# Attention's value products moved from one tile of keys to two behind the transposes, and a block's output split by ScalarE and VectorE out of PSUM

## The chip, the cores and the metric

The kernel runs on one core of a Trainium2 chip. The metric is the device time of one execution in microseconds. Three runs of the kernel before took 2472.91, 2474.02 and 2474.15 us; the median is 2474.02 us. A profiled execution is one run of its own.

Engines are named as in the profile: PE is TensorE's matmul, PEld its weight load, DVE is VectorE, ACT is ScalarE, POOL is GpSimd, and SP the engine whose queue issues nearly all DMAs.

## The reference, cut to what matters

The model has two layers at a width of 1024 on 1024 tokens, all in float32. Layer 0 mixes by attention, layer 1 by an mLSTM, and each is followed by a SwiGLU feed-forward network. The change touches layer 0's attention alone:

```python
h = h + nsa_swa_mixer(rmsnorm(h, norm_mix[0]), ...)   # 8 NSA heads and 8 sliding-window heads, 2 key heads each
# for each block of 128 queries, NSA (gates g0, g1, g2 per head):
p_c = masked_softmax(q @ kc.T * scale, ...)    # 63 compressed keys
p_s = masked_softmax(q @ ksel.T * scale, ...)  # top 16 of 16 key blocks of 64: all causal keys here
p_w = masked_softmax(q @ kwin.T * scale, ...)  # the last 512 keys
o_a = g0 * (p_c @ vc) + g1 * (p_s @ vsel) + g2 * (p_w @ vwin)
# sliding window with sinks, span of 256 keys:
e = exp(logits - max(logits.max(), sink));  p = e / (e.sum() + exp(sink - max))
o_b = p @ v
out = concat(o_a, o_b) @ w_out
```

## The kernel before

A float32 product is made of two parts that TensorE takes, `hi` (the value cast to fp32r) and `lo` (what is left). A dense product is three matmuls per 128x128 weight: hi by hi, hi by lo, lo by hi (lines 188 to 190 while attention runs). Splitting a tile costs one cast (ACT or POOL) and one subtraction (DVE).

**Blocks.** Attention runs over 32 blocks. A block is one kind (1: window with sinks, 0: NSA), one key head g (4 query heads share it) and one tile n of 128 queries. First come the 16 sink blocks, then 16 NSA blocks, n from 0 to 3 for either g, then 4 to 7. A sink block has one unit of work; an NSA block has three: the compressed keys, the n+1 tiles of selected keys, and up to 5 tiles of the window.

**A unit** passes through three steps, each one unit behind the one before, in `blocks()`: `scores` (line 592; queries times keys into PSUM tile S, then mask and maximum by DVE on line 643, then the exponential by ACT on line 652 into tile e), `weights` (line 665; POOL scales e by gate over sum, line 684), and `values` (line 686). So while unit i's scores are made, unit i-2's values are.

**Values.** For each tile of 128 keys, PE transposes four 128x128 pieces of e into a PSUM tile T (line 701), ACT casts T into `eh` (line 705), DVE subtracts to get the low part `el` (line 706, shown as eh too), and PE multiplies both by the values into the block's accumulator `po` (lines 695 and 696). The values sit as hi and lo side by side in the 128 columns of the stationary operand, so `po` holds the hi product in partitions 0 to 63 and the lo product in 64 to 127. `late` holds the products of one tile back until the next tile's transposes have been issued. The last tile's products of a unit are made at the start of the next unit's loop.

**Output.** `outputs()` (line 713) copies `po` out of PSUM by ACT (`oc`, line 716), and POOL makes three instructions of it: the hi part of the upper half (line 117), the rest of it (line 720) and that plus the lower half (line 721). Two DMAs store both parts to `os` in DRAM (line 724).

**Order.** The Tile layer schedules each engine's queue by its own model and inserts the semaphores. `pinned` keeps an instruction behind all that was traced before it on its engine; the first transpose of a tile and both products are pinned. Each engine runs its queue in order. A tile tag with `bufs` names at most so many live tiles; the packer then gives each tile an address, and a tile may reuse the address of any dead one, of another tag too. A new tile waits for the last readers of what lay there, DMAs included.

**Dense work beside.** A list `beside` in `mixer_ab` gives generators of dense products (the rest of the input projection, then the output projection `ab_out`), each with a position at which its loads are issued and a stretch of positions over which its steps are spread. A position is the number of the block and the share of it that has been traced. `ab_out` reads back what `outputs()` stored.

After block 31 the last quarter of the output projection and the first two tiles of the feed-forward network (`ffn_head`) follow, then a chain of vector work that makes the operands of the big feed-forward products.

```python
ec = self.page("w", "ec", w=256)                       # 625
eh, el = self.pair("k", "eh")                          # 704
if late: products(*late)                               # 707
c = self.page("w", "oc"); t = self.page("w", "ot"); o = self.page("w", "o", F32R)   # 715 to 718
```

Of the kernel before, what the change touches and what calls it, by code (L numbers as in the profile page):

```python
# [20 lines left out]
OP = mybir.AluOpType  # L21
# [15 lines left out]
class Net:  # L37
# [554 lines left out]
    def scores(self, q, unit, g, n):  # L592
# [21 lines left out]
        if br == 0:  # L614
            p = tile()
            for r in range(4):
                products(p, 64 * r, r)
            yield st, es
            s = p[:, :256].rearrange("p (r k) -> p r k", r=4)
            nc.vector.tensor_tensor(s, s, mask[:, None, :].to_broadcast([P, 4, 64]), op=OP.add)  # L620
            nc.vector.tensor_reduce(nm, s, AX.X, OP.max, negate=True)
            if n == 0:

                nc.vector.tensor_scalar(nm, nm, 1e20, None, op0=OP.min)
            ec = self.page("w", "ec", w=256).rearrange("p (r k) -> p r k", r=4)
            for r in range(4):
                nc.scalar.activation(ec[:, r], s[:, r], AF.Exp, bias=nm[:, r:r + 1], accum_out=l[:, r:r + 1])
                es.append(ec[:, r])
            yield st, es
            return  # L630
# [52 lines left out]
        for r in range(4):  # L683
            self.last_scale = nc.gpsimd.tensor_scalar(es[r][:, :w], es[r][:, :w], f[:, r:r + 1], 0.0, op0=OP.mult, op1=OP.add)  # L684

    def values(self, unit, es, po, first, last):


        nc = self.nc
        br, _, w, _, vals = unit  # L690
        n = min(P, w)
        late = None

        def products(j, v, eh, el):
            self.pinned(nc.tensor.matmul(po, v[:n], eh[:n], start=first and j == 0, stop=False))  # L695
            self.pinned(nc.tensor.matmul(po, v[:n], el[:n], start=False, stop=last and j == len(vals) - 1))  # L696

        for j, v in enumerate(vals):
            tp = self.tmp_ps("T")
            for r in range(4):  # L700
                t = nc.tensor.transpose(tp[:n, r * P:(r + 1) * P], es[r][:, j * P:j * P + n], self.ident)  # L701
                if r == 0:
                    self.pinned(t)
            eh, el = self.pair("k", "eh")
            nc.scalar.copy(eh[:n], tp[:n])  # L705
            nc.vector.tensor_tensor(el[:n], tp[:n], eh[:n].bitcast(F32), op=OP.subtract)  # L706
            if late:
                products(*late)
            late = j, v, eh, el
            yield  # L710
        yield lambda: products(*late)

    def outputs(self, kind, g, n, po):
        nc = self.nc
        c = self.page("w", "oc")
        nc.scalar.copy(c, po)  # L716
        t = self.page("w", "ot")
        o = self.page("w", "o", F32R)
        self.hi_copy(o[0:64], c[0:64], "pool")
        nc.gpsimd.tensor_tensor(t[64:128], c[0:64], o[0:64].bitcast(F32), op=OP.subtract)  # L720
        nc.gpsimd.tensor_tensor(o[64:128], c[64:128], t[64:128], op=OP.add)
        r0 = (kind * 8 + 4 * g) * 64
        for i in range(2):
            nc.sync.dma_start(self.os[i, r0:r0 + 256, n * P:(n + 1) * P].rearrange("(r d) q -> d r q", d=64),
                              o[64 * i:64 * i + 64].bitcast(F32).rearrange("d (r q) -> d r q", r=4))

    def blocks(self, todo):
# [7 lines left out]
                work.append((b, k, k == len(sizes) - 1))  # L735
                pos.append((i + sum(sizes[:k]) / sum(sizes), size / sum(sizes)))
        pos += [(len(todo) + i, 1) for i in range(2)]
        qs, done, late = {}, [], None

        def ahead(i):  # L740
            if i < len(todo):
# [4 lines left out]
        for i in range(len(work) + 2):  # L746
            tiles, sc = iter(()), iter(())
            per = 1
            if i > 1:
                b, k, last = work[i - 2]  # L750
                unit = done[i - 2][2]
                if k == 0:
                    po = self.acc("po")
                tiles = self.values(unit, done[i - 2][1], po, k == 0, last)
                per = -(-len(unit[4]) // 4)
            if i < len(work):
                b, j, _ = work[i]
# [4 lines left out]
            if 0 < i <= len(work):  # L762
                st, es, u = done[i - 1]
                self.weights(u, work[i - 1][0][1], work[i - 1][0][2], st, es)
            res, end = None, None
            self.attn = "sinks" if pos[i][0] < 24 else "nsa"
            for r in range(5):
                res = next(sc, res)
                if r == 0 and late:
                    late()  # L770
                    late = None
                for k in range(per):
                    x = next(tiles, None)
                    if callable(x):
                        end = x
                    yield pos[i][0] + pos[i][1] * (r * per + k + 1) / (5 * per)
            for x in tiles:
                if callable(x):
                    end = x
            for res in sc:  # L780
                pass
            if i < len(work):
                done.append((*res, us[j]))
            if end:
                def late(end=end, args=work[i - 2][0], po=po, last=work[i - 2][2]):
                    end()
                    if last:
                        self.outputs(*args, po)
        late()

    def mixer_ab(self):
        nc, tc = self.nc, self.tc
# [2 lines left out]
        with tc.tile_pool(name="at", bufs=1) as self.at:  # L795
# [21 lines left out]
            def parts():  # L817
                for c in range(NC):
                    with self.tc.issue_after(self.last_scale.ins):
# [4 lines left out]
            beside = [(0.0, 0.0, 13.6, 80, second), (14.0, 14.0, 17.8, 16, third),  # L824
                      (18.0, 18.6, 26.4, 32, self.ab_out(range(4, 8), (0, 1))),
                      (26.9, 27.8, 31.0, 17, squares(self.ab_out(range(0, 4), (0,)))),
                      (31.8, 32.4, 33.9, 9, self.ab_out(range(0, 2), (1,))), (32.4, 32.4, 33.9, 8, parts())]
            done = [0] * len(beside)
            for at in self.blocks(todo):
                for i, (load, start, end, steps, gen) in enumerate(beside):  # L830
# [768 lines left out]
```

## Time and profile before

| | |
|---|---|
| runs shown, median (lowest to highest) | 2474.02 us (2472.91 to 2474.15) |
| the profiled execution: its own time, its span | 2475.77 us, 2474.00 us |
| PE busy | 2374.9 us, 96% |
| DVE, ACT, POOL busy | 1630.4 us (66%), 896.7 us (36%), 501.9 us (20%) |
| TensorE's granted clock, mean | 0.982 |
| first transposes of e for values, last `po` product | 100.1 us, 649.8 us |

The span is what the profile covers; 1.77 us of the execution's own time lie outside it. Attention with the dense work beside it fills about 80 to 650 us of the span. A matmul's end is modelled, so PE counts as busy in part of a wait; a weight load (PEld) is issued for each matmul ahead of it, and a wait for an operand shows on PEld first. The granted clock is the share of full speed (2.4 GHz; the other level is 1.2 GHz) over a stretch.

### The profile page before, as it was taken

How to read it: one execution, taken by the hardware profiler on the slowest of the kernel's cores; microseconds unless marked ns; L12 is line 12 of the kernel's file. 1: busy time of each engine (PE TensorE's matmuls, PEld its weight loads, DVE VectorE, ACT ScalarE, POOL GpSimd, SP SyncE). 2: the span in 40 equal slices, each digit the busy share in tenths (PEclk: the TensorE clock that was granted, in tenths of full speed). 3: DMA queues.
4: the chain of work that ended last, by engine and by line, in shares of the span. 5: the costliest groups of instructions: out<-in, count | busy, mean ns of one | idle time of the engine just before them, and what ended most of it. 6: DMA issues, size and time to landing. Idle time of an engine off the chain costs nothing.

```text
span 2474.0 us, 29578 instructions
## 1 busy us (share of the span) xinstructions
PE 2374.9 (96%) x10729; PEld 1895.6 (77%) x10729; DVE 1630.4 (66%) x2817; ACT 896.7 (36%) x1851; POOL 501.9 (20%) x606
## 2 busy tenths in 40 slices
PE   7999998998889999999999999999979999999998
PEld 5778776776668888887777788887868888887886
DVE  6546666688786666668876554544487656667867
ACT  5234565576353223222222344332263222322222
POOL 3135654444300000002322111111100000002322
PEclk9999999999989999999999999999989999999999
DMA  5623642311434443449333211112143434348433
GB/s 190 196 69 111 199 123 60 89 45 37 136 99 139 134 132 124 155 152 323 127 134 101 65 43 39 39 56 102 40 144 107 154 108 165 128 162 300 139 140 115
DMA packets 246757, 304.20 MB, mean 123 GB/s; under 512 B 19076, under 2 KB 157524, under 8 KB 246612
## 3 DMA queue, kind: packets, MB, share of 16 engines
q1 hardware_dynamic: 246612, 302.31, 37.8%
q8 instruction: 85, 1.39, 0.2%
q14 instruction: 60, 0.49, 0.1%
HBM read 218.33 MB, written 83.90 MB: 122 GB/s over the span
## 4 chain that ended last, share of the span: by engine, by line
PE 67%; DVE 6%; issue 4%; POOL 4%; ACT 2%; DMA 1%; SPq 0%; DVEq 0%; POOLq 0%; ACTq 0%
PE dn L1173 14%; PE wb L993 10%; PE wb L994 10%; PE wb L995 10%; PE acc L181 4%; PE acc L180 4%; PE acc L179 4%; POOL e L684 1%; PE T L701 1%; PE S L610 1%; DVE y L124 1%; POOL x L245 1%; PE po L695 1%; PE po L696 1%; PE pr L995 1%
## 5 line engine op out<-in xcount | busy, mean ns | idle before, releaser
L993 PE MATMUL wb<-y,wh 128*128 128x512 f32 x1120 | 442.6, 395 | 6.1 <-ACT wh L119 4.8
L994 PE MATMUL wb<-y,wh 128*128 128x512 f32 x1120 | 442.7, 395 | 0.0
L995 PE MATMUL wb<-y,wh 128*128 128x512 f32 x1120 | 441.0, 394 | 0.0
L117 POOL TENSOR_SCALAR wo<-ws 128x1024 fp32r<-128x1024 f32 x84 | 121.3, 1456 | 1099.2 <-DVE m L1061 437.7
L993 PEld LDWEIGHTS wb<-y,wh 128*128 128x128 f32 x1120 | 210.8, 188 | 58.8 <-ACT wh L119 5.2
L995 PEld LDWEIGHTS wb<-y,wh 128*128 128x128 f32 x1120 | 211.1, 188 | 49.7 <-DVE wh L124 0.7
L994 PEld LDWEIGHTS wb<-y,wh 128*128 128x128 f32 x1120 | 210.9, 188 | 48.1
L1173 PE MATMUL dn<-xo,wo 128*128 128x512 f32 x924 | 220.1, 400 | 6.6 <-DVE wo L124 6.1
L1173 PE MATMUL dn<-wo,xo 128*128 128x512 f32 x924 | 215.7, 395 | 0.6 <-ACT xo L119 0.3
L1173 PEld LDWEIGHTS dn<-xo,wo 128*128 128x128 f32 x924 | 176.7, 192 | 49.9 <-DVE wo L124 7.4
L1173 PEld LDWEIGHTS dn<-wo,xo 128*128 128x128 f32 x924 | 173.7, 188 | 42.5 <-DVE xo L124 1.1
L179 PE MATMUL acc<-x,whl 128*128 128x512 f32 x416 | 170.1, 409 | 0.0
L180 PE MATMUL acc<-x,whl 128*128 128x512 f32 x416 | 166.1, 399 | 0.0
L181 PE MATMUL acc<-x,whl 128*128 128x512 f32 x416 | 165.3, 397 | 0.0
L188 PE MATMUL acc<-x,whl 128*128 128x512 f32 x384 | 157.6, 410 | 4.6 <-DMA x<-os 2.5
L684 POOL TENSOR_SCALAR e<-e,st 128x256 f32<-128x256 f32 (+7 forms) x192 | 122.2, 656 | 173.2 <-ACT oc L716 33.4
L189 PE MATMUL acc<-x,whl 128*128 128x512 f32 x384 | 155.1, 404 | 1.9 <-DVE x L246 1.0
L119 ACT CAST xo<-hb 128x1024 fp32r<-128x1024 f32 x84 | 79.4, 976 | 206.0 <-PE dn L1173 134.8
L190 PE MATMUL acc<-x,whl 128*128 128x512 f32 x384 | 153.2, 399 | 0.7 <-DVE whl L124 0.7
L706 DVE TENSOR_TENSOR eh<-T,eh 128x512 fp32r<-128x512 f32 (+1 forms) x178 | 120.3, 687 | 44.8 <-ACT eh L705 43.6
L124 DVE TENSOR_TENSOR wh<-ws,wh 128x512 fp32r<-128x512 f32 x136 | 92.8, 686 | 83.6 <-ACT wh L119 83.5
L610 PE MATMUL S<-kv,qa 128*128 128x256 f32 (+3 forms) x528 | 123.8, 331 | 11.5 <-ACT e L652 3.8
(334 smaller groups left out, 4415.8 us busy)
## 6 DMA issues: line engine op xcount, KB each, us to landing
ws<-in_ffn_w_down SPq DMA_DIRECT2D x34, 1024.0 KB
ws<-in_ffn_w_gate SPq DMA_DIRECT2D x22, 1024.0 KB
ws<-in_ffn_w_up SPq DMA_DIRECT2D x22, 1024.0 KB
sd<-m SPq DMA_DIRECT2D x22, 1024.0 KB
hs<-m SPq DMA_DIRECT2D x80, 256.0 KB
qa<-qs SPq DMA_DIRECT2D x128, 128.0 KB
hb<-hs SPq DMA_DIRECT2D x16, 1024.0 KB
ws<-sd SPq DMA_DIRECT2D x16, 1024.0 KB
```

The lines of the kernel that those rows point to most:

```text
L179: nc.tensor.matmul(ps, w[:, 0, k], xh, start=(start and k == 0), stop=False)
L180: nc.tensor.matmul(ps, w[:, 0, k], xl, start=False, stop=False)
L181: nc.tensor.matmul(ps, w[:, 1, k], xh, start=False, stop=(stop and k == n - 1))
L188: self.nc.tensor.matmul(ps, w[:, 0, i], xh, start=i == 0, stop=False)
L189: self.nc.tensor.matmul(ps, w[:, 0, i], xl, start=False, stop=False)
L190: self.nc.tensor.matmul(ps, w[:, 1, i], xh, start=False, stop=i == len(xs) - 1)
L610: nc.tensor.matmul(p[:, at + c:at + c + k.shape[1]], qq[:, r * P:(r + 1) * P], k, start=i == 0, stop=i == 1, skip_group_check=True)
L684: self.last_scale = nc.gpsimd.tensor_scalar(es[r][:, :w], es[r][:, :w], f[:, r:r + 1], 0.0, op0=OP.mult, op1=OP.add)
L993: nc.tensor.matmul(ps, t[:, 0, k], xh, start=first and k == 0, stop=False, skip_group_check=True)
L994: nc.tensor.matmul(ps, t[:, 0, k], xl, start=False, stop=False, skip_group_check=True)
L995: nc.tensor.matmul(ps, t[:, 1, k], xh, start=False, stop=last and k == 3, skip_group_check=True)
L1173: nc.tensor.matmul(ps[i], l, r, start=first and k == 0 and q == 0, stop=end and k == 10 and q == 2, skip_group_check=True)
```

## The change

`values` no longer keeps the products back itself. It puts each tile's products on a list `pending` that belongs to all of attention, and once more than two are on it, the oldest is made. So the products stand two tiles of keys behind the transposes, and the distance holds across units and blocks. `outputs` is called when a block's last product is made, and what is on the list at the end is made after the loop.

`outputs` reads `po` in PSUM directly: ACT casts the upper half to `o`, DVE subtracts that from the upper half, and DVE adds the lower half. POOL has no part in it, and `oc` is gone.

The tiles change place: `eh` and `el` become one tile of a tag of their own with 6 bufs, which the output's `o` and `t` share; `ec` moves to the tag `e`. One position in `beside` changes from 31.8 to 32.3.

```diff
-            ec = self.page("w", "ec", w=256).rearrange("p (r k) -> p r k", r=4)
+            ec = self.pg.tile([P, 2 * PAGE], F32, name="ec", tag="e", bufs=EB)[:, :256].rearrange("p (r k) -> p r k", r=4)
...
-    def values(self, unit, es, po, first, last):
+    def values(self, unit, es, po, first, last, pending, after):
...
             self.pinned(nc.tensor.matmul(po, v[:n], el[:n], start=False, stop=last and j == len(vals) - 1))
+            if last and j == len(vals) - 1:
+                after()
...
-            eh, el = self.pair("k", "eh")
+            t = self.pg.tile([P, 2, PAGE], F32R, name="eh", tag="eh", bufs=6)
+            eh, el = t[:, 0, :H5], t[:, 1, :H5]
             nc.scalar.copy(eh[:n], tp[:n])
             nc.vector.tensor_tensor(el[:n], tp[:n], eh[:n].bitcast(F32), op=OP.subtract)
-            if late:
-                products(*late)
-            late = j, v, eh, el
+            pending.append(lambda j=j, v=v, eh=eh, el=el: products(j, v, eh, el))
+            if len(pending) > 2:
+                pending.pop(0)()
             yield
-        yield lambda: products(*late)

     def outputs(self, kind, g, n, po):
         nc = self.nc
-        c = self.page("w", "oc")
-        nc.scalar.copy(c, po)
-        t = self.page("w", "ot")
-        o = self.page("w", "o", F32R)
-        self.hi_copy(o[0:64], c[0:64], "pool")
-        nc.gpsimd.tensor_tensor(t[64:128], c[0:64], o[0:64].bitcast(F32), op=OP.subtract)
-        nc.gpsimd.tensor_tensor(o[64:128], c[64:128], t[64:128], op=OP.add)
+        t = self.pg.tile([P, 2, PAGE], F32R, name="ot", tag="eh", bufs=6)
+        o, t = t[:, 0, :H5], t[:, 1, :H5].bitcast(F32)
+        nc.scalar.copy(o[0:64], po[0:64])
+        nc.vector.tensor_tensor(t[64:128], po[0:64], o[0:64].bitcast(F32), op=OP.subtract)
+        nc.vector.tensor_tensor(o[64:128], po[64:128], t[64:128], op=OP.add)
...
-                tiles = self.values(unit, done[i - 2][1], po, k == 0, last)
+                tiles = self.values(unit, done[i - 2][1], po, k == 0, last, pending, lambda b=b, po=po: self.outputs(*b, po))
...
-        late()
+        for late in pending:
+            late()
...
-                      (31.8, 32.4, 33.9, 9, self.ab_out(range(0, 2), (1,))), (32.4, 32.4, 33.9, 8, parts())]
+                      (32.3, 32.4, 33.9, 9, self.ab_out(range(0, 2), (1,))), (32.4, 32.4, 33.9, 8, parts())]
```

PE's order in NSA block 24 (kind 0, g = 0, n = 4), kernel before. `T_4151`, whose parts are `eh_4156` and `eh_4157`, is the tile transposed before `T_4167`:

```order
L701 MATMUL T_4167<-consts_80,e_4049 128x128
L610 MATMUL S_4207<-kv_1428,qa_3719 128x512
L695 MATMUL po_4058<-eh_4156,kv_1431 128x512
L610 MATMUL S_4207<-kv_1428,qa_3719 128x512
L610 MATMUL S_4207<-kv_1428,qa_3719 128x128 x2
L696 MATMUL po_4058<-eh_4157,kv_1431 128x512
L701 MATMUL T_4178<-consts_80,e_3989 128x128
```

The same place in the changed kernel. `eh_4007` comes from the tile two before `T_4035`, `eh_4030` from the one after that; lines 702, 694 and 695 are 701, 695 and 696 of before:

```order
L702 MATMUL T_4035<-consts_80,e_3912 128x128
L694 MATMUL po_3921<-eh_4007,kv_1413 128x512
L695 MATMUL po_3921<-eh_4007,kv_1413 128x512
L610 MATMUL S_4062<-kv_1410,qa_3590 128x512
L610 MATMUL S_4062<-kv_1410,qa_3590 128x128 x2
L610 MATMUL S_4080<-kv_1410,qa_3590 128x512 x2
L702 MATMUL T_4045<-consts_80,e_3855 128x128
```

A tile's transposes and four 512-column matmuls of other tiles' products now stand between a tile's own transposes and its products, where before one tile's transposes and two such matmuls stood.

POOL's order at the end of block 23 (output `o_4077`), kernel before:

```order
L684 TENSOR_SCALAR ec_3951<-ec_3951,st_3928 128x64 x4
L117 TENSOR_SCALAR o_4077<-oc_4074 64x512
L684 TENSOR_SCALAR e_3989<-e_3989,st_3984 128x512
L684 TENSOR_SCALAR e_4006<-e_4006,st_3984 128x512
L684 TENSOR_SCALAR e_4032<-e_4032,st_3984 128x512
L684 TENSOR_SCALAR e_4049<-e_4049,st_3984 128x512
L720 TENSOR_TENSOR ot_4076<-oc_4074,o_4077 64x512
L721 TENSOR_TENSOR o_4077<-oc_4074,ot_4076 64x512
L684 TENSOR_SCALAR e_4070<-e_4070,st_4065 128x512
```

In the changed kernel POOL goes from one scaling to the next there, and the two output instructions (`ot_4012`) stand in DVE's order, between two low parts of `eh`:

```order
L708 TENSOR_TENSOR eh_4007<-T_4002,eh_4007 128x512
L719 TENSOR_TENSOR ot_4012<-po_3717,ot_4012 64x512
L720 TENSOR_TENSOR ot_4012<-po_3717,ot_4012 64x512
L681 TENSOR_TENSOR st_3992<-st_3992,misc_356 128x4
L708 TENSOR_TENSOR eh_4030<-T_4025,eh_4030 128x512
L708 TENSOR_TENSOR eh_4040<-T_4035,eh_4040 128x512
```

Both output instructions wait for ACT's cast of the same block, which waits for the block's last product on PE; the low parts of the next block's second and third tile are queued behind them.

## Rows read from the trace of the kernel before

**Rows 1.** The page: busy time by engine, and the clock in 40 slices.

```profile
PE 2374.9 (96%) x10729; PEld 1895.6 (77%) x10729; DVE 1630.4 (66%) x2817; ACT 896.7 (36%) x1851; POOL 501.9 (20%) x606
...
PEclk9999999999989999999999999999989999999999
```

**Rows 2.** Windows by stage: start and end, length, busy PE, PEld, DVE, ACT, POOL, clock, DMA.

```profile
80.00:275.00 195.00, 188.73 (x928) 150.84 (x926) 108.17 (x297) 76.91 (x219) 79.74 (x105) 0.98 0.45 128
...
350.00:450.00 100.00, 89.96 (x451) 70.73 (x451) 60.64 (x159) 52.69 (x155) 43.65 (x72) 0.91 0.29 80
450.00:550.00 100.00, 94.57 (x521) 74.96 (x520) 75.53 (x156) 65.34 (x156) 47.48 (x62) 0.98 0.24 67
550.00:650.00 100.00, 89.56 (x449) 68.59 (x448) 80.55 (x150) 57.31 (x118) 47.01 (x56) 0.95 0.18 54
```

**Rows 3.** Waits of PEld, 80 to 660: who for whom, total us, times, longest.

```profile
PEld po L696 <- DVE eh L706: 19.3, 53, 1.5
PEld po L695 <- ACT eh L705: 13.2, 36, 1.3
PEld S L610 <- ACT e L652: 12.2, 25, 1.8
PEld T L701 <- POOL e L684: 5.4, 13, 0.9
...
PEld po L695 <- ACT e L652: 4.1, 2, 3.5
...
PEld T L701 <- ACT e L652: 2.6, 2, 2.1
```

**Rows 4.** Waits of PE itself, 80 to 660.

```profile
PE po L696 <- DVE eh L706: 6.6, 11, 1.0
...
PE po L695 <- ACT e L652: 3.9, 2, 3.4
PE po L695 <- ACT eh L705: 3.3, 7, 1.0
PE T L701 <- ACT e L652: 2.7, 3, 1.9
...
PE T L701 <- POOL e L684: 1.7, 5, 0.6
```

**Rows 5.** Groups by line and shape, 80 to 660: busy us, mean ns, idle before.

```profile
L720 POOL TENSOR_TENSOR ot<-oc,o 64x512 f32<-64x512 f32 x32 | 45.2, 1412 | 2.7
L721 POOL TENSOR_TENSOR o<-oc,ot 64x512 fp32r<-64x512 f32 x32 | 43.1, 1348 | 2.5
...
L706 DVE TENSOR_TENSOR eh<-T,eh 128x512 fp32r<-128x512 f32 x162 | 109.4, 688 | 43.6 <-ACT eh L705 42.4
...
L705 ACT CAST eh<-T 128x512 fp32r<-128x512 f32 x162 | 94.1, 589 | 78.2 <-PE T L701 74.5 <-DVE r L956 1.6 <-issue 1.3
```

**Rows 6.** Waits of ACT, 80 to 660; then ACT and PE in time, 428 to 434.

```profile
ACT e L652 <- POOL o L721: 14.9, 5, 3.8
...
432.74 0.80 ACT L652 ACTIVATE e<-S,st 128x640 f32<-128x640 f32 x1 [3.55 <-DMA os<-o]
...
433.68 0.79 PE L695 MATMUL po<-eh,kvc 64*128 64x512 f32 x1 [3.36 <-ACT e L652]
```

**Rows 7.** Windows of 10 us after 350, columns as in rows 2.

```profile
430.00:440.00 10.00, 6.64 (x31) 5.33 (x31) 3.77 (x10) 4.22 (x14) 3.13 (x4) 0.66 0.60 147
...
480.00:490.00 10.00, 7.07 (x35) 5.42 (x34) 4.98 (x11) 4.93 (x16) 8.29 (x10) 0.83 0.48 133
...
620.00:630.00 10.00, 6.37 (x26) 4.72 (x27) 6.04 (x8) 2.15 (x4) 9.90 (x12) 0.78 0.51 148
```

**Rows 8.** PE and POOL in time at the last two outputs, and DVE beside the last.

```profile
625.28 0.50 PE L188 MATMUL acc<-x,whl 128*128 128x512 f32 x1 [2.49 <-DMA x<-os]
...
664.04 0.51 PE L189 MATMUL acc<-x,whl 128*128 128x512 f32 x1 [0.72 <-DMA x<-os]
...
618.31 1.27 POOL L720 TENSOR_TENSOR ot<-oc,o 64x512 f32<-64x512 f32 x1
...
652.58 2.99 POOL L720 TENSOR_TENSOR ot<-oc,o 64x512 f32<-64x512 f32 x1
...
654.34 1.77 DVE L956 SCALAR_TENSOR_TENSOR r<-r,consts 128x512 f32<-128x512 f32 x1
```

More of the change, by code (lines that the diff above doesn't have):

```diff
@@ L691, in values @@
         n = min(P, w)
-        late = None
         def products(j, v, eh, el):
@@ L737, in blocks @@
         pos += [(len(todo) + i, 1) for i in range(2)]
-        qs, done, late = {}, [], None
+        qs, done, pending = {}, [], []
         def ahead(i):
@@ L764, in blocks @@
                 self.weights(u, work[i - 1][0][1], work[i - 1][0][2], st, es)
-            res, end = None, None
+            res = None
             self.attn = "sinks" if pos[i][0] < 24 else "nsa"
@@ L768, in blocks @@
                 res = next(sc, res)
-                if r == 0 and late:
-                    late()
-                    late = None
                 for k in range(per):
-                    x = next(tiles, None)
-                    if callable(x):
-                        end = x
+                    next(tiles, None)
                     yield pos[i][0] + pos[i][1] * (r * per + k + 1) / (5 * per)
-            for x in tiles:
-                if callable(x):
-                    end = x
+            for _ in tiles:
+                pass
             for res in sc:
@@ L783, in blocks @@
                 done.append((*res, us[j]))
[L784 to L789, printed above, removed]
+        for late in pending:
+            late()
     def mixer_ab(self):
```

## The prediction

> **What bounds the kernel now.** The page comes first: PE is busy for 96% of the span, and its clock stands at 9 in nearly every slice [rows 1]. No change that leaves PE its matmuls can win much, and this one leaves them. What can be won is idle PE time and clock. The windows by stage, read next, show where: while the input projection fills in (80 to 275) PE loses 6 of 195 us, but in the 100 us from 350 it is busy for 90 at a clock of 0.91, and in the 100 us from 550 for 89.6 at 0.95 [rows 2]. DVE climbs from 61 to 81 us of each 100 in those stages. So the loss lies in the NSA blocks, where a unit is long and little dense work is left.
>
> The waits say on whom. A weight load shows a wait first, so I read PEld and then PE. On PEld the two products wait 19.3 us for DVE's low part (53 times) and 13.2 us for ACT's cast (36 times); the scores wait 12.2 us for ACT's exponential, since their PSUM tile is still being read; the transposes wait 5.4 us for POOL's scaling and 2.6 for ACT [rows 3]. Of this PE itself stands idle 6.6 and 3.3 us at the products, and 3.9, 2.7 and 1.7 us behind ACT or POOL [rows 4]. The first number is too high as a gain, because a weight load also waits in time that PE still fills; the second is too low, because a matmul's end is modelled. The truth lies between, and I keep both ends.
>
> **A. Products two tiles back.** The cast takes 0.59 us and the subtraction 0.69 [rows 5], so 1.28 us pass at least between a tile's last transpose and its second product. PE starts 521 matmuls in the 100 us from 450 [rows 2], 0.19 us for one. Six matmuls (four transposes, two products) thus cover some 1.15 us before the change: a little less than is needed, which fits 89 waits at a mean of 0.37 us, 32.5 us in all, among 178 tiles. Twelve cover 2.3 us. That is a margin of 1 us, and no wait of the two kinds is over 1.5 [rows 3]. Bounds: at the low end the 9.9 us that PE stands idle (6.6 + 3.3); at the high end the 32.5 us less the 0.04 us that I allow each of 89 loads as an ordinary step, 28.7. Below nothing it can fall only if the wait comes back elsewhere and longer, which is a rival. I take half of 28.7, **14 us**, because part of it returns: matmuls that no longer wait reach the next score tile earlier, and the exponential for which that waits (12.2 us) isn't made faster.
>
> **B. The output leaves POOL.** POOL's share of a block's output is two instructions of 1.41 and 1.35 us and one smaller [rows 5], between scalings that later transposes wait for. Worse is what ACT does: its exponential writes a tile that lies where an old output lay, and it waits for POOL's last output instruction five times, 14.9 us in all; at 432.74 it waits 3.55 us for the output's DMA, and PE's first product of the block behind it 3.36 us [rows 6]. With the output in the tag of `eh`, the exponential has no such predecessor. PE's idle time of this kind is 3.9 + 2.7 + 1.7 = 8.3 us [rows 4]; by PEld it is 4.1 + 2.6 + 5.4 = 12.1 [rows 3]; if other predecessors take over, half of the first, 4. I take **8 us**, the lines of PE, since these waits are long enough to show there.
>
> **C. The clock.** In the windows of 10 us the granted clock is 0.66 from 430, 0.83 from 480 and 0.78 from 620 [rows 7], a mix of the two levels, and two of these stand at long PE waits shown here: 3.36 us at 433.68 [rows 6] and 2.49 at 625.28 [rows 8]. A window at 0.66 does 6.6 us of full-speed work in 10; the three lose 3.4 + 1.7 + 2.2 = 7.3 us. Bounds: 0, and what the three stages lose in all, 9 + 2 + 5 = 16 [rows 2]. I take **5 us**: the first and most of the third, as their waits go or shrink.
>
> **D. The way through DRAM.** The last pieces of the output projection read what the last blocks stored: PE waits 2.49 us at 625.28 and 0.72 at 664.04 for that load [rows 8]. POOL's three instructions take 1.41 + 1.35 + about 0.7 (an estimate: half of the first) = 3.5 us; two on DVE at 0.69 (the nearest row, another subtraction from PSUM of 512 columns [rows 5]) take 1.4. ACT's copy stays as a cast. The store leaves some 2 us sooner, and the products two tiles later give 1.15 of it back. Bounds 0 and 3.2; I take **1.7 us**. The load's position 32.3 for 31.8 puts an SP issue later, before stores that it would otherwise stand ahead of; I count it at nothing, because the load can't run before those stores.
>
> **E. What is added.** DVE gets 2 x 32 instructions, 64 x 0.69 = 44 us; ACT keeps its count; POOL loses 96. DVE has 19 us free in 100 in its fullest stage [rows 2], so most is hidden by its idle time. But DVE works in order, and the two stand ahead of the next block's low parts. Bounds: 0, and 1.38 us at each of 16 NSA blocks, 22. I take the last four blocks, where DVE is fullest: **5 us**. If DVE had no idle time there, the whole 22 would count.
>
> The Trainium skill ("SBUF — State Buffer", section "SBUF: two separate sides") has a rule that touches this: GpSimd and VectorE share a port pair, which a GpSimd instruction or a VectorE instruction with two SBUF inputs holds alone for its whole length. The trace agrees once: POOL's subtraction took 2.99 us with such a DVE instruction of 1.77 us beside it, and 1.27 without [rows 8]. By it 96 holders of the pair go, and the new DVE instructions, with one input in PSUM, aren't any; should every DVE instruction beside them have lost what that POOL instruction lost, E would be a gain.
>
> **Sum.** 14 + 8 + 5 + 1.7 - 5 = 23.7 us off the profiled execution's 2475.77: 2452.1. That execution stands 1.75 above the median of the runs shown, so **2450 us**. Its own range is 2434 (A and C near their high ends) to 2466 (A and B at their low ends, C at nothing, E at its 5).
>
> **Rivals.**
>
> *The waits only move (2467).* If not latency but the pace of cast and subtraction sets PE's wait, two tiles of distance give nothing: T's PSUM buffers are no more than before, and a transpose then waits for DVE where a product did. For it: DVE at 81% late, and its low parts idle before them only behind ACT. Against: in the rows of before no transpose waits for `eh`, and DVE has idle time in each stage. A is then 0, D stays, and so do about 6 of B and 4 of C, with 5 for E: 7 us. The Trainium skill ("Perfetto Trace Analysis", section "Optimization Strategy") says that a bubble that repeats can mean too few buffers for the next tile; by that this rival would hold, and the trace of before, with its waits on the value and not on a tile, does not bear it out.
>
> *DVE stalls at each block's end (2481 to 2500, slower).* The two output instructions wait in DVE's queue for ACT's cast, and this for the block's last product, which PE now makes behind two more tiles of transposes. Behind them stand the next tiles' low parts and, in the NSA blocks, the masks of the next scores. With about 1 us of wait and 1.38 of work that is 2.4 us for each of 16 blocks, 38 us; with A lost and B, C and D at 12 it makes 2474 + 26 = 2500; in half of the blocks 19 - 12 gives 2481. For it: DVE's queue in order and DVE's load. Against: products are pinned in an order in which ACT's cast can be ready before DVE gets there, and a margin of 1 us from A absorbs as much of each stall. It decides once a stall takes over 0.75 us (12 / 16) of PE in each NSA block.
>
> *All ends high (2428).* A 28.7, B 12, C 7.3, D 3, less 5: 46 us. For it: the waits are short and even, as a latency's are. Against: the exponential's 12.2 us remain behind them.
>
> *Half of the change doesn't do what it says (2461).* Outputs now take one of six `eh` tiles and hold it until their DMAs end, and the exponential's tile may still lie over something that a DMA reads. Then B is nothing and C 2: 14 + 2 + 1.7 - 5 = 13 us. For it: the wait for DMA at 432.74 came from a reuse of addresses, and addresses are chosen anew. Against: outputs come once in a block, six tiles are many.
>
> **How the numbers follow.** Likeliest case 0.48; waits only move 0.18; slower 0.12; all high 0.10; half of the change 0.12; each with its own spread of some 10 us. I take 0.2% (4.9 us) as the least that a measurement tells from no change: faster is below 2469.1, slower above 2479.0. Faster: 0.47 + 0.09 + 0.10 + 0.09 = 0.75. Same: 0.01 + 0.08 + 0.03 = 0.12. Slower: 0.01 + 0.12 = 0.13. The range 2430 to 2476 leaves out the slower case, half of the high one and little more, near 0.2.
>
> **What would show it.** In the changed kernel's waits, PEld's 32.5 us at the products fall under 6, and the scores' 12.2 stay within 4 of that: A. ACT's exponential no longer waits for an output, and the 3.4 us stop before a block's first product is gone: B. The windows 430 to 440 and 620 to 630 stand above 0.9: C. PE's waits on the output's load halve: D. DVE's busy time rises by 44 us, POOL's falls by about 110 (32 x 3.5): E. I am wrong if transposes wait for DVE's `eh` (the first rival), if DVE shows idle time of some 1 us ahead of the output's subtraction at each block with PE waiting soon after (the second), or if ACT still waits for DMAs of outputs (the last).

## The result: 36 us faster, and the profile after

The changed kernel takes 2437.07 us (median of 4 runs, 2436.52 to 2437.70) against 2473.47 for the kernel before, run beside it: a ratio of 0.9861, 95% interval 0.9846 to 0.9877. The prediction had 2450. The profiled execution took 2436.71 us with a span of 2434.9, 39.1 us less than the span before.

The page of the changed kernel, busy time by engine and the clock in 40 slices, answers to [rows 1]:

```profile
PE 2350.0 (97%) x10729; PEld 1882.4 (77%) x10729; DVE 1655.9 (68%) x2881; ACT 897.0 (37%) x1851; POOL 396.7 (16%) x510
...
PEclk9999999999999999999999999999989999999999
```

PE has as many matmuls as before. DVE has 64 instructions more, POOL 96 fewer and 105 us less work. Of the two slices at 8 in [rows 1] the first, the twelfth (680 to 742 us), is a 9 now.

The windows by stage of the changed kernel (columns as in [rows 2]):

```profile
80.00:275.00 195.00, 192.89 (x967) 156.13 (x966) 124.77 (x333) 81.14 (x238) 36.89 (x73) 0.99 0.47 132
350.00:450.00 100.00, 97.34 (x546) 80.05 (x546) 80.30 (x195) 63.42 (x175) 35.43 (x66) 1.00 0.36 96
450.00:550.00 100.00, 96.98 (x553) 78.95 (x552) 88.96 (x179) 71.20 (x163) 36.22 (x52) 1.00 0.19 54
550.00:650.00 100.00, 86.91 (x399) 64.40 (x398) 78.55 (x141) 49.04 (x92) 29.28 (x38) 0.95 0.33 96
```

In the 100 us from 350 PE starts 546 matmuls where it started 451, at a clock of 1.00 where it had 0.91. DVE is busy for 80 and 89 us of 100 there, more per time than before, and still PE hardly waits. The last window holds another piece of the work now, since attention ends 29 us sooner.

Its waits of PEld from 80 to 660, the part that answers to [rows 3]:

```profile
PEld S L610 <- ACT e L652: 18.1, 30, 1.7
PEld T L702 <- POOL e L684: 7.5, 22, 1.0
PEld T L702 <- DVE eh L708: 4.4, 9, 2.3
...
PEld acc L189 <- DMA x<-os: 2.2, 1, 2.2
...
PEld po L695 <- DVE eh L708: 1.0, 3, 0.5
...
PEld po L694 <- ACT eh L707: 0.2, 1, 0.2
```

And its waits of PE itself, as in [rows 4]:

```profile
PE S L610 <- ACT e L652: 8.2, 13, 1.3
PE T L702 <- POOL e L684: 2.3, 5, 0.8
...
PE T L702 <- DVE eh L708: 1.9, 1, 1.9
...
PE acc L189 <- DMA x<-os: 1.8, 1, 1.8
```

The 32.5 us of waits at the products are 1.2. Of ACT's exponential waiting for an output, or a first product for that exponential, no row is left. What came instead is smaller, though not nothing: transposes wait 4.4 us for a low part and 2.1 us more for POOL's scaling (7.5 for 5.4), and the scores 5.9 us more for ACT's exponential (18.1 for 12.2), all as weight loads show it.

**Where the 39 us are.** Windows between places of the program show it best, since the same work lies in them in either kernel: attention (first score to last product), the tail up to the first of the feed-forward network's main products, these up to the first down product, and from there to the mLSTM's first `pn` product. Before:

```profile
83.21:649.82 566.61, 531.25 (x2718) 418.54 (x2717) 378.07 (x919) 300.37 (x805) 265.47 (x375) 0.97 0.36 101
649.82:723.83 74.01, 64.18 (x245) 47.67 (x243) 57.70 (x91) 34.30 (x57) 8.54 (x8) 0.93 0.46 142
723.83:1121.52 397.69, 392.24 (x1682) 316.77 (x1680) 266.40 (x424) 116.47 (x210) 5.09 (x4) 0.99 0.43 139
1121.52:1421.13 299.61, 289.27 (x1226) 230.08 (x1226) 214.83 (x251) 76.38 (x107) 81.61 (x73) 0.98 0.43 148
```

The changed kernel:

```profile
85.30:621.17 535.87, 513.53 (x2717) 411.04 (x2717) 413.29 (x986) 300.66 (x805) 160.46 (x282) 0.99 0.37 105
621.17:689.55 68.38, 61.13 (x244) 45.94 (x243) 53.70 (x87) 34.56 (x57) 3.19 (x6) 0.98 0.48 150
689.55:1088.77 399.22, 392.34 (x1681) 315.93 (x1680) 264.96 (x424) 117.14 (x210) 4.11 (x4) 0.99 0.41 140
1088.77:1383.52 294.75, 284.86 (x1227) 226.70 (x1227) 213.27 (x252) 76.16 (x107) 84.41 (x73) 0.99 0.43 148
```

Attention is 30.7 us shorter: PE's idle time there, length less busy, falls from 35.4 to 22.3, by 13 us, and the clock rises from 0.97 to 0.99. The tail is 5.6 us shorter, 2.6 of it idle time, and the clock there went from 0.93 to 0.98. The last stretch is 4.9 us shorter with the same idle time (10.3 and 9.9): nothing there was edited, only its clock is higher. The rest of the span takes 2.1 us more, nearly all of it ahead of the first score (85.30 us for 83.21), where the clock is 0.98 for 1.00.

The mean granted clock of the whole span is 0.982 before and 0.990 after. (1 - 0.982) x 2474.0 = 44.5 us were lost to it before, (1 - 0.990) x 2434.9 = 24.3 after: 20 us, good to some 2 us with means of three digits. As a share of the gain that is more likely too high than too low. Of the 15 executions of the kernel before that ran beside the first experiments, the one with a clock of 0.980 took 2477.97 us and the one with 0.986 took 2466.87: 11.1 us for 14.8 us of lost clock, three quarters. So **an estimated 15 to 20 of the 39 us are clock, and the rest, 19 to 24, are waits**. PE's idle time over the whole span, 99.1 us before and 84.9 after, shows 14.2 us of these; the others would lie in time that counts as busy, since a matmul's end is modelled.

### The profile page after: what moved, and what is told of

Read it like the earlier page. It is cut to its first block, busy times and chain, and to the rows that moved or that the text cites. A ratio compares the mean times of both kernels' runs of the same rounds, so it can differ in the third digit from the quotient of the medians.

```text
span 2434.9 us, 29574 instructions
## 1 busy us (share of the span) xinstructions
PE 2350.0 (97%) x10729; PEld 1882.4 (77%) x10729; DVE 1655.9 (68%) x2881; ACT 897.0 (37%) x1851; POOL 396.7 (16%) x510
## 4 chain that ended last, share of the span: by engine, by line
PE 64%; DVE 7%; issue 2%; DMA 1%; POOL 1%; ACT 1%; SPq 0%; DVEq 0%; ACTq 0%; POOLq 0%
PE dn L1162 14%; PE wb L982 10%; PE wb L983 10%; PE wb L984 10%; PE acc L181 4%; PE acc L180 4%; PE acc L179 4%; DVE y L124 1%; DVE r L945 1%; DVE x L246 1%; PE pn L1503 1%; PE pr L984 1%; DMA hb<-hs 1%; POOL x L245 1%; PE pr L982 1%
## 5 line engine op out<-in xcount | busy, mean ns | idle before, releaser
L117 POOL TENSOR_SCALAR wo<-ws 128x1024 fp32r<-128x1024 f32 x84 | 127.3, 1528 | 1087.4 <-DMA ws<-in_ffn_w_down 933.0
L119 ACT CAST wh<-ws 128x512 fp32r<-128x512 f32 x136 | 83.5, 616 | 132.1 <-DMA ws<-in_ffn_w_gate 127.5
```

Source lines behind the costliest of these rows:

```text
L117: nc.gpsimd.tensor_scalar(out, in_, 1.0, 0.0, op0=OP.mult, op1=OP.add)
L119: nc.scalar.copy(out, in_)
```

## The experiments

Each kernel ran in alternation with the kernel before; the ratio is against that. Idle time and clock in the table are those of the attention stretch (first score to last product) of the profiled execution, idle being its length less PE's busy time there; "clock of span" is the mean of the whole. The kernel before's own median moved by 2.7 us between the comparisons, so medians of rows from different ones compare to some 3 us.

| kernel | median, us | ratio (95%) | PE idle | clock | clock of span |
|---|---|---|---|---|---|
| before | 2470.8 to 2473.5 | 1 | 35.4 | 0.97 | 0.982 |
| distance two, POOL output, pages | 2473.62 | 1.001 (1.000 to 1.002) | 48.2 | 0.96 | 0.982 |
| same, POOL's output work cut to one instruction | 2449.69 | 0.9906 (0.9890 to 0.9923) | 27.9 | 0.97 | 0.983 |
| distance two, POOL output, own tag | 2461.51 | 0.9958 (0.9943 to 0.9973) | 33.8 | 0.96 | 0.983 |
| distance two, new output, pages | 2449.79 | 0.9918 (0.9905 to 0.9932) | 26.2 | 0.98 | 0.986 |
| distance one, new output, own tag | 2457.59 | 0.9955 (0.9943 to 0.9968) | 25.6 | 0.98 | 0.987 |
| distance one, new output, pages | 2461.09 | 0.9966 (0.9953 to 0.9978) | 25.8 | 0.97 | 0.986 |
| distance one, POOL output, own tag | 2490.61 | 1.0070 (1.0052 to 1.0087) | 44.6 | 0.95 | 0.978 |
| changed | 2437.07 | 0.9861 (0.9846 to 0.9877) | 22.3 | 0.99 | 0.990 |
| changed, distance three | 2438.34 | 0.9862 (0.9841 to 0.9883) | 23.6 | 0.98 | 0.988 |
| changed, distance one in the last block | 2432.85 | 0.9840 (0.9826 to 0.9855) | 18.4 | 0.99 | 0.992 |

Two parts of the change no run takes back by themselves, the load's position and the place of `ec`. The position is 32.3 in every kernel here but the kernel before, "distance one, new output, pages" and "distance one, POOL output, own tag"; and `ec` lies in the tag `e` in all but the first two of these three. So what is called the distance below, where a row is set against the kernel before, has these two in it.

**1. The output back on POOL.** The values' tiles go back to pages too; `ec` and the load's position stay as changed.

```diff
-            t = self.pg.tile([P, 2, PAGE], F32R, name="eh", tag="eh", bufs=6)
-            eh, el = t[:, 0, :H5], t[:, 1, :H5]
+            eh, el = self.pair("k", "eh")
...
-        nc.scalar.copy(o[0:64], po[0:64])
-        nc.vector.tensor_tensor(t[64:128], po[0:64], o[0:64].bitcast(F32), op=OP.subtract)
-        nc.vector.tensor_tensor(o[64:128], po[64:128], t[64:128], op=OP.add)
+        nc.scalar.copy(c, po)
+        self.hi_copy(o[0:64], c[0:64], "pool")
+        nc.gpsimd.tensor_tensor(t[64:128], c[0:64], o[0:64].bitcast(F32), op=OP.subtract)
+        nc.gpsimd.tensor_tensor(o[64:128], c[64:128], t[64:128], op=OP.add)
```

> The changed kernel with the block's output by ACT's copy and three POOL instructions again, in the pages of the kernel before; the low parts go back to pages of the tag k, since with their own tag this doesn't fit SBUF. The products stay two tiles back. Theory 1 (the distance carries most of the 36 us, the output some 10): 2448 us, products' waits on PEld under 5 us as in the changed kernel, ACT's exponential waiting for POOL's output or its DMA again. Theory 2 (the output carries most): 2462 us or more. Theory 3 (the tiles' places carry it): near 2470.

2473.62 us: in pages and with POOL's output the distance is worth nothing. Theory 1 missed by 25 us; the time fits theory 2 and theory 3, which experiments 4 and 5 put to the test. The waits at the products did go (5.8 us by PEld for the low part), but others took their place. In time, POOL of this kernel behind the output of a block:

```profile
407.72 0.61 POOL L117 TENSOR_SCALAR o<-oc 64x512 fp32r<-64x512 f32 x1
408.41 1.30 POOL L720 TENSOR_TENSOR ot<-oc,o 64x512 f32<-64x512 f32 x1
409.79 1.28 POOL L721 TENSOR_TENSOR o<-oc,ot 64x512 fp32r<-64x512 f32 x1
411.16 1.18 POOL L684 TENSOR_SCALAR ec<-ec,st 128x64 f32<-128x64 f32 x4
```

ACT, then DVE, then PE at the same place:

```profile
411.10 0.58 ACT L706 CAST eh<-T 128x512 fp32r<-128x512 f32 x1 [2.66 <-POOL o L721]
```

```profile
412.38 0.83 DVE L643 CUSTOM_DVE_ANT_0 S<-S,misc 128x640 f32<-128x640 f32 x1 [3.12 <-POOL ec L684]
413.13 0.14 DVE L643 DVE_READ_ACCUMULATOR2_ANT st<- 128x1 f32 x1
413.13 0.69 DVE L707 TENSOR_TENSOR eh<-T,eh 128x512 fp32r<-128x512 f32 x1
```

```profile
413.87 0.66 PE L702 MATMUL T<-consts,e 128*128 128x128 f32 x4 [2.93 <-DVE eh L707]
```

POOL's work on an output, 3.2 us almost without a pause, ends at 411.07. ACT's cast of the next tile has waited 2.66 us for it, since its tile takes a place that the output's chain had; DVE's mask has waited 3.12 us for the scaling queued behind the output; and PE stands still for 2.93. No distance between transposes and products covers a cast that doesn't start. At the tail PE waits for the load of the late output:

```profile
PE acc L188 <- DMA x<-os: 10.0, 1, 10.0
```

**2. The same with POOL's chain cut short.** One instruction in place of three; the low half of the output's split is left out.

```diff
-        self.hi_copy(o[0:64], c[0:64], "pool")
-        nc.gpsimd.tensor_tensor(t[64:128], c[0:64], o[0:64].bitcast(F32), op=OP.subtract)
-        nc.gpsimd.tensor_tensor(o[64:128], c[64:128], t[64:128], op=OP.add)
+        self.hi_copy(o, c, "pool")
```

> The first ablation (distance two, a block's output by ACT's copy and POOL, pages) with POOL's three output instructions, 0.6 + 1.3 + 1.3 us, replaced by one of 0.6 to 0.8 us that only copies: the low half of the output's split is left out. Theory 8 (the length of POOL's work on the output is what keeps ACT's casts and, through the scaling behind it, DVE's masks waiting): most of the 24 us between that ablation (2473.6) and the kernel with pages and the new output (2449.8) come back, 2450 to 2460, and the waits of casts for POOL's output (7.3 us) and of masks for POOL's scaling (10.4 us) fall to a third. Theory 9 (any output that passes through a copy and another engine comes late; its length is a side issue): 2466 to 2474.

2449.69 us, just under the range of theory 8, which holds; so theory 9 doesn't. ACT's and DVE's waits for POOL's output and scalings, from 80 to 660 us, in the first ablation:

```profile
ACT eh L706 <- POOL o L721: 7.3, 3, 2.7
...
DVE S L643 <- POOL ec L684: 8.7, 3, 3.1
DVE S L643 <- POOL e L684: 1.7, 1, 1.7
```

and with the short chain, whose one instruction takes 629 ns:

```profile
ACT eh L706 <- POOL o L117: 1.0, 2, 0.8
...
DVE S L643 <- POOL e L684: 0.7, 1, 0.7
DVE S L643 <- POOL ec L684: 0.4, 2, 0.2
```

From 17.7 us to 2.1, and PE's idle time from 48.2 to 27.9. It was the length of POOL's work that cost the 24 us, not the copy or the hop between engines: the kernel with the new output in pages takes 2449.79 us, no less than this one.

**3. The distance back to one tile.**

```diff
-            if len(pending) > 2:
+            if len(pending) > 1:
```

> The changed kernel with products one tile behind the transposes (across blocks), the new output and the new places kept. Theory 1 (distance): the products' waits on PEld are back at 25 to 33 us, and the time is 2458 to 2463 us. Theory 2 (output carries most): 2440 to 2447. The pace of cast and subtraction as the limit (a rival of the prediction): within 5 us of the changed kernel, 2437 to 2442, since the waits would only stand at another instruction.

2457.59 us, 20.5 more than the changed kernel, just under the time that theory 1 gave. The products' waits come back, though at half of the size that it gave; the waits of PEld in this kernel:

```profile
PEld S L610 <- ACT e L652: 22.5, 27, 3.5
PEld po L695 <- DVE eh L708: 12.5, 42, 0.7
...
PEld po L694 <- ACT eh L707: 2.2, 6, 1.0
```

14.7 us where 32.5 stood before. The other half is not POOL's: in the kernel before no row has a cast waiting for POOL's output, and experiment 4's kernel, without POOL in the output, still has 26.4 us. What took it lies among the rest that sets this kernel apart from experiment 4's: the values' tiles in their own tag, the distance kept across units and blocks, `ec` and the load's position. No run separates these. The ends of units alone are not it: in the order of the weight loads of the kernel before, the 64 pairs of products (of 178) that come at the end of a unit, ahead of the next tile's transposes, have only 5 of the 32.5 us. That the pace of cast and subtraction sets the limit is refuted: the distance is worth 20 us here.

**4. The new output alone, on the kernel before.**

```diff
-        c = self.page("w", "oc")
-        nc.scalar.copy(c, po)
...
-        self.hi_copy(o[0:64], c[0:64], "pool")
-        nc.gpsimd.tensor_tensor(t[64:128], c[0:64], o[0:64].bitcast(F32), op=OP.subtract)
-        nc.gpsimd.tensor_tensor(o[64:128], c[64:128], t[64:128], op=OP.add)
+        nc.scalar.copy(o[0:64], po[0:64])
+        nc.vector.tensor_tensor(t[64:128], po[0:64], o[0:64].bitcast(F32), op=OP.subtract)
+        nc.vector.tensor_tensor(o[64:128], po[64:128], t[64:128], op=OP.add)
```

> The kernel before with the new output alone (ACT's cast, DVE's two instructions out of PSUM, no copy), in pages of the tag w as before; the products stay one tile back within a unit. Theory 1: 10 us faster than before, 2463, with the products' 32 us of waits as they were. Theory 2: 2445 to 2450. If the outputs' place and not their engine made ACT's exponential wait: 2470, and ACT waits for DMAs of outputs still.

2461.09 us, 9.7 less than before in that comparison, as theory 1 had it. Most of the waits at the products are left:

```profile
PEld po L696 <- DVE eh L706: 15.8, 50, 1.9
PEld po L695 <- ACT eh L705: 10.6, 35, 0.7
```

So in pages the parts don't add: the distance (with `ec` and the load's position) gives nothing, the output alone 10, both 21 (next). Theory 2 is refuted too.

**5. The places.** First the changed kernel with the values' tiles in pages (the first three lines of the first diff alone), then the kernel before with the own tag and `ec` in tag `e`, then POOL's output inside the own tag (12 single pages).

> The changed kernel with the low parts' tiles in pages of the tag k again; order, distance and output as changed. Theory 1: 2437 us, as the changed kernel, within 5. Theory 3 (the own tag of six tiles matters): 2445 or more, with PE or ACT waiting for addresses.

> The kernel before with the low parts in their own tag of six pairs and ec in the tag e; order, distance and output as before. If places by themselves are worth something (as the 12.7 us between the changed kernel and the one with pages suggest): 2458 to 2464. If places only matter once the products stand two tiles back: 2468 to 2473, as before.

> The changed kernel with a block's output by ACT's copy and POOL's three instructions, and with all its tiles in the tag of the low parts (12 single pages in place of 6 pairs), so that no exponential or cast takes the place of a dead output. Theory 4 (POOL's three instructions stand between a block's scalings, and through them DVE's masks, the casts and the transposes run late; places are a side issue): 2462 to 2473, with DVE's masks waiting for POOL's scaling and 8 to 10 us of PE's wait for the load of the last output. Theory 5 (with the first ablation the casts waited for POOL's output by the reuse of its place): 2442 to 2450.

2449.79, 2490.61 and 2461.51 us. The own tag is worth 12.7 us in the changed kernel; with `ec`'s move it costs 18 in the kernel before, which no expectation had. There the waits of ACT for POOL's output, 14.9 us in 5 [rows 6], became

```profile
ACT e L652 <- POOL o L722: 23.8, 8, 3.8
```

8 waits for 5, as if more of the exponential's tiles lay on outputs; the trace has no addresses to show it. In the third kernel that row is gone, yet casts wait for outputs inside their own tag:

```profile
ACT eh L706 <- POOL o L719: 9.8, 3, 3.6
```

and masks for POOL's scaling, 6.3 us. Theory 4 and theory 5 both hold a part. The time lies at theory 4's end, but PE waits 3.1 us for the last outputs' loads, not 8 to 10. At a distance of two, POOL's way out costs 24 us in either set of places (2473.62 for 2449.79 in pages, 2461.51 for 2437.07 in the own tag). The distance is another matter: the third kernel is 29 us faster than the second, and both have POOL's output and an own tag, though not the same places for the output; in pages it gave nothing. Places thus carry a third of the gain, the part of theory 3 that holds. Whichever tile takes an output's place, the 3.2 us of POOL are waited for; where the places fall decides by whom. Of the 12.7 us only 4.4 lie in attention (540.3 us there against 535.9); 4.3 are the clock between the first down product and the mLSTM (299.1 us against 294.75), with the same idle time.

**6. Three tiles.** `len(pending) > 3`, and eight pairs.

> The changed kernel with products three tiles back and eight pairs. Theory 1 (a latency of 1.3 us, covered by two tiles): no gain, 2435 to 2440; the output then comes a tile later and the wait for the last load at the tail grows by about 1 us. If two tiles still leave a part of the wait: 2430 or less.

2438.34 us, as theory 1 had it, though PE's wait for the last load didn't grow. With 8 pairs and the distance at two the time was 2440.59 us, ratio 0.9872 (0.9857 to 0.9888):

> The changed kernel with eight pairs for the low parts and the output instead of six. If PE's 4.4 us of waits of transposes for DVE's low part come from a lack of pairs: 2433 to 2435. If six are enough: 2436 to 2440.

The transposes' waits for a low part are no lack of pairs: with eight they are 4.4 us, 9 times, as with six. The Trainium skill ("Perfetto Trace Analysis", section "Optimization Strategy") has it that a bubble that repeats can mean too few buffers; no run here shows that for these waits.

**7. Does the clock follow the waits?** Extra casts of the same tile, in 8 blocks:

```diff
+            for _ in range(7 if br == 1 and j == 1 and len(vals) > 4 else 1):
-            nc.scalar.copy(eh[:n], tp[:n])
+                nc.scalar.copy(eh[:n], tp[:n])
```

> The changed kernel with the cast of the second tile of selected keys made seven times over (the same result) in the 8 NSA blocks of more than four tiles: six casts of 0.58 us, 3.5 us of ACT, of which about 1 us is covered by the distance and more by the exponentials' slack, so that PE stands idle 10 to 20 us longer in all. Theory 6 (the granted clock falls where PE has stood idle, so that a wait costs about double): the time lost to the clock grows by at least half of the added idle time, with the granted clock's mean at 0.985 or less, and the kernel takes 2455 to 2475 us. Theory 7 (the clock's drops fall by chance and not behind waits): clock 0.988 to 0.991 as before, and 2447 to 2457.

2444.01 us: 48 more casts, 27 us of ACT's time, cost only 7 us, under both ranges, so most was covered. Attention in this kernel, to be set beside the changed kernel's row above:

```profile
84.88:625.62 540.74, 514.82 (x2717) 411.94 (x2716) 413.06 (x985) 322.20 (x853) 160.14 (x281) 0.98 0.36 103
```

Idle time grew by 3.6 us, and the clock fell from 0.99 to 0.98; over the span it is 0.988, 29.3 us lost to it instead of 24.3. This doesn't decide between the theories. 5 us of clock for 3.6 of idle time, in one profiled execution, is what theory 6 had in kind; but the clock is 0.988, which lies in theory 7's range and not under theory 6's 0.985. The stall was too well covered to tell. The ends of the table (0.95 with 44.6 us idle, 0.99 with 18.4) go with theory 6, the first ablation, with the most idle time (48.2) at 0.96, less so; that clock and waits go together isn't yet that one makes the other. Nor does it settle the second half. There the changed kernel with 12 extra transposes after attention kept the changed kernel's clock:

> The changed kernel with 12 extra transposes of a constant after attention's last product, some 1 to 3 us of PE's time whose result is not used; all behind it only moves later. If the 5 us that the second half gained are due to where its short stalls fall against the drops of the granted clock: 2440 to 2446, and the clock of some windows between 1000 and 1450 us falls under 1 again. If they are due to the order or places of the work: 2438 to 2440, the clock there as in the changed kernel.

2440.51 us, a time that both cases allow, and 294.79 us between the first down product and the mLSTM, as in the changed kernel. So this shift, by some 2 us, doesn't bring those drops back. Why this stretch takes 299 us in some of the kernels and 295 in others, with equal idle time, stays open.

**8. A version that beats both.** The output of the last block is read back by dense work that waits for it.

```diff
-            if len(pending) > 2:
+            while len(pending) > self.depth:
...
+                self.depth = 1 if b == todo[-1] else 2
```

> The changed kernel with the products one tile behind in the last block alone, so that its output comes a tile sooner. If the tail is bound by the way of the last output through DRAM: 2434 to 2436. If by DVE's queue there: 2437 to 2440, no gain.

2432.85 us (2431.19 to 2433.93), all its runs under all of the changed kernel's, though the two intervals overlap. Attention ends 6.9 us sooner in the profiled execution (it starts 1.5 us sooner), and the waits for `os` are gone from its tail; its row of the attention stretch:

```profile
83.83:614.28 530.45, 512.03 (x2717) 409.84 (x2716) 407.67 (x979) 301.00 (x805) 160.24 (x281) 0.99 0.37 105
```

## Why the prediction was right, and which term was mis-sized

The forecast, 24 us faster, stood for 36; the sign, the bound (idle PE time and clock) and the likeliest case's own range held. By its terms, against the 39 us of the profiled executions:

- **C, the clock, -5: the term that was mis-sized, and the step that failed.** By the means of the span it came to some -20 (44.5 - 24.3 us), of which 15 to 20 showed in time. The step counted three windows of 10 us, and credited "the first and most of the third". The first two did go, and so did what it hadn't counted, three windows of the kernel before in which no wait of PE was over 1.5 us:

```profile
350.00:360.00 10.00, 9.85 (x47) 7.60 (x46) 5.07 (x19) 5.07 (x23) 3.99 (x10) 0.83 0.65 184
360.00:370.00 10.00, 8.52 (x39) 6.51 (x40) 5.74 (x20) 5.07 (x18) 6.18 (x10) 0.81 0.30 84
370.00:380.00 10.00, 10.00 (x48) 8.30 (x47) 6.30 (x18) 4.84 (x17) 2.62 (x7) 0.85 0.17 50
```

The stages from 350 and 450 run at 1.00 now, where they lost 9 and 2 us. The third did not go: the stage from 550 is at 0.95 in both kernels, and the drop at the wait for the output's load is there still, now in the window from 590, in the changed kernel:

```profile
580.00:590.00 10.00, 7.64 (x35) 4.87 (x33) 6.69 (x18) 6.62 (x14) 5.57 (x6) 0.84 0.00 1
590.00:600.00 10.00, 7.82 (x35) 5.95 (x34) 8.75 (x12) 3.03 (x6) 9.10 (x11) 0.82 0.56 133
```

No wait of PE in these two is over 1.9 us: in these windows and the three above the clock fell without a long wait. Attention as a whole gained 12 us of clock (0.97 of 566.6 us, 0.99 of 535.9), within the step's bound of 16; the tail and the second half, which the step left out, some 8, of which the last 5 have no cause in the change that a run shows; the opening took 2 back.
- **A + B + D + E, -18.7.** The span's gain less the clock's is 19 to 24. The sum is near; two of its parts are so for other reasons than stated, which is luck.
- **A, -14, and B, -8,** were sized as if either stood alone. They don't: in pages the distance is worth 0 with POOL's 3.2 us per output in the way (experiment 1) and some 11 with the new output (experiment 4 against experiment 5's first kernel), `ec` and the load's position included; in the own tag, with the new output, it is worth 20.5, clock included. B is worth 9.7 at a distance of one in pages and 24 at a distance of two. The step "a latency of 1.28 us against 1.15 us of cover" is right in that two tiles take the products' waits away and three give nothing more. But its cover doesn't explain who waited: the pairs at the ends of units, with no transposes between, waited least, and experiment 3 brought back only half. (The high end is 32.5 - 89 x 0.04 = 28.9, not 28.7; between a tile's transposes and its products stand now the transposes of two tiles, as the twelve matmuls of the step have it, and not of one.) One sign failed: the scores' wait was to stay within 4 of 12.2 us and is 18.1.
- **D, -1.7.** PE's waits for the output's load went from 2.49 + 0.72 us [rows 8] to 1.85 + 0.34, 1 us; they were to halve. Experiment 8 shows that the distance itself holds the last output back: taken away in one block, it gives 4 us more.
- **E, +5.** DVE's two instructions take what the step said, and hardly wait. By line and shape in the changed kernel (busy us, mean ns, idle before):

```profile
L720 DVE TENSOR_TENSOR ot<-po,ot 64x512 fp32r<-64x512 f32 x32 | 22.2, 695 | 1.0
L719 DVE TENSOR_TENSOR ot<-po,ot 64x512 f32<-64x512 f32 x32 | 21.9, 683 | 1.7 <-ACT ot L718 0.7
```

44.1 us in all, as worked out, with 2.7 us of idle time ahead of them. What they cost on the path no run separates: PE's transposes wait 1.9 us for DVE, and the scores wait longer for an exponential that in turn waits longer for DVE's mask (45.5 us for 38.3). Experiment 2's short chain, with no output work on DVE, is no faster than the new output in pages, so it can't be much. DVE's busy time grew by less than 44 us (35 in attention, 25.5 in all), in part because others got shorter: the split of `qf` (two operands in SBUF) took 924 ns before and 707 after. It took 812 to 924 in the four kernels with POOL's three instructions and 703 to 708 in the ten without them. The Trainium skill's rule on the port that GpSimd and VectorE share ("SBUF — State Buffer", section "SBUF: two separate sides") agrees with that, and the low parts, which read PSUM, stayed at 0.69 us.

The rivals: the waits that only move came to 4.4 us of 32.5 at the transposes, and 5.9 more at the scores; DVE's stall at a block's end to 0.7 us once in 32; and outputs that still hold ACT up are in no row of the changed kernel. The case "all ends high" (2428) was the nearest of them, but its clock term, 7.3, was too small as well. By its own terms the low end of the likeliest case's range comes to 2463 and not 2466, which changes nothing.

## What to carry to other kernels

Two waits in one chain needn't add: before crediting the removal of one, look whether the instruction that ends it is itself held by the other. A block's closing work on a slow engine is waited for by whoever takes its place or stands behind it in a queue, so its length counts even when that engine is idle 80% of the time. Where tiles lie is a change of its own, worth as much here as either of the others, and has to be tested by itself. And where the granted clock is under 1, bound its term by all that the stages lose, and not from the windows with a long wait alone: here the clock gave about as much as the waits, though what makes it fall isn't settled.

## What the runs showed that was not expected

About half of the 39 us came as granted clock, part of it in a stretch in which nothing was edited. Three instructions of 0.6 to 1.3 us on an engine that is busy 20% of the span made two other engines stop for 3 us at one block's end, and cutting them to one gave back 24 us. And a tag of its own for a tile pair was worth 13 us in one kernel and, with `ec`'s move, cost 18 in another; that where dead tiles left room decides it is a reading of the waits, not shown.
